# Dots and sums of fetched expert rows, issued on VectorE in the program's order

## The chip, the cores and the metric

The kernel runs on one core of a Trainium2 chip. The metric is the device time of one execution in microseconds (us). The kernel before took 3069.17 us, the median of three runs (3067.21 to 3079.47).

## The reference

The kernel computes a two-layer backbone over 256 latent tokens and 256 context tokens of width 1024. A layer mixes tokens (gated linear attention and neighbourhood attention, merged by gates) and then channels. The channel mixing is what the change touches. It is a retrieval of single-neuron experts (PEER): each token scores 8 heads x 2 x 128 keys, and each head picks 16 of the 16384 experts, so a token has 128 experts in all.

```python
def block(xb):                                # 128 tokens
    ...                                       # qb, s, top 16, cand, top 16: experts, g
    u = jnp.take(expert_u, experts, axis=0)   # (tokens, 128, 1024)
    v = jnp.take(expert_v, experts, axis=0)
    act = jax.nn.gelu(jnp.einsum('td,ted->te', xb, u))
    return jnp.einsum('te,ted->td', act * g, v)
```

The last layer gives out the latent stream alone, so the context stream goes through PEER in layer 0 only, while the latent stream does so in both layers.

## The kernel before, in words

**Two ways of PEER.** For the latent stream the kernel computes all 16384 hidden activations densely on TensorE (`hidden`, L325) and multiplies them by a matrix A that holds the gate of each chosen expert and zero elsewhere. `build` makes A in three chunks from one-hot marks: on VectorE oi (L951), oj (L953) and two products oa (L956) for every 8 tokens, on TensorE their products (L964), on ScalarE the copy into A (L966). `scale` multiplies activations by A in place (L1017), and `value` multiplies the result by expert_v (L1051). `peer_prep` (L915 to L931) lays out the indices and gates ahead of the first chunk.

For the context stream of layer 0 the kernel fetches the chosen rows instead. This is `gather`. For each of 128 expert places and both blocks of 128 tokens, an indirect DMA that GpSimd issues (L1173) brings one row of 1024 numbers to each token's partition, first all rows of expert_u, then all of expert_v: 2 x 256 fetches. A fetched u row is multiplied by the token's normed input hN and added up on VectorE (the dots, L1180, in place in the row's buffer gx). After the last dot a gelu and the gates give the coefficients coef. A fetched v row is scaled by its coefficient and added to the running result vsum (the sums, L1189; the first of each block is L1187). At the end vsum is multiplied by a broadcast row (L1194) and added to the context x (L1195), from which layer 1 starts. There are six buffers for fetched rows (gx=6), and the fetch of a row is written four rows ahead of its dot or sum (lead=4).

**The loops and their weaving.** `gather` is a generator that yields after each row; two yields for hN come first. The program runs it in three places beside work on the latent stream. In the mixer of the latent stream it takes five rows at each of 17 steps, after the heads of the context stream are done. In the head stage of the latent stream (query, scores, top 16 of eight heads, with the hidden activations of eight of the 32 groups) it takes three rows at each of ten steps. In `peer_out`, the loop over 32 groups of 512 experts, it takes 400/224 rows at each of the 224 steps. An iteration of that loop scales the group's activations, computes the hidden activations of the group four further on (four steps, in iterations 4 to 27) and the value products (four steps). The second and third chunk of A are built beside iterations 4 to 7 and 16 to 19. What is left of `gather` is run ahead of iteration 31.

**What sets the order.** The kernel is written on a tile framework that fixes each engine's order of instructions when the program is built. It plays the program through with times of its own for instructions and transfers, and on each engine it issues what is ready by then, the earliest in the program first. On the chip each engine takes its instructions in that fixed order and waits, where an operand isn't there yet, at the instruction that needs it. Dots and sums are free in this: one whose row has come, by those times, is issued ahead of VectorE work that stands before it in the program and isn't ready. The order of fetches on GpSimd's queue is the program's, and a fetch waits until one of the six buffers is free. Weights are loaded by SP into four buffers (w) and two more (dw), a tile of 512 KB each.

The method `keep_in_program_order` of the framework takes an instruction and adds an edge to it: it is issued after the instruction of its engine that the program wrote just before it. The edge is one of order; it adds no semaphore and no wait for an end. Instructions that the program writes later may still be issued ahead of it.

Of the kernel before, what the change touches and what calls it, by code (L numbers as in the profile page):

```python
# [17 lines left out]
OP = mybir.AluOpType  # L18
# [51 lines left out]
class Net:  # L70
# [1073 lines left out]
    def gather(self, l, s, st):  # L1144


        nc, gp = self.nc, self.gp
        si = 0 if s == "l" else 1
        n, lead = self.n["gx"], self.n["lead"]
        sh, sc = (self.modT[l][:, 24 + 8 * i:32 + 8 * i, si] for i in range(2))  # L1150
        g = gp.tile([128, 8], F32, name="gcol", bufs=1)
        nc.vector.scalar_tensor_tensor(g, sc, 1.0, self.colv[f"gn2{l}"], op0=OP.add, op1=OP.mult)
        rows = [self.wtile([128, D]) for i in range(2)]
        for row, col in zip(rows, (g, sh)):
            self.row_of([row[:, 0:512], row[:, 512:D]], col)
        def room(name):
            return [self.pe.tile([128, D], F32, name=name, tag="hp", bufs=self.n["hp"]) for b in range(2)]
        hN, sums = room("hn"), None
        for b in range(2):
            nc.vector.scalar_tensor_tensor(hN[b], self.x[s, b], self.rs[s][:, b:b + 1], rows[0], op0=OP.mult, op1=OP.mult)  # L1160
            nc.vector.tensor_tensor(out=hN[b], in0=hN[b], in1=rows[1], op=OP.add)
            yield
        idx = st["idx"].rearrange("p b h r -> p b (h r)")
        coef = gp.tile([128, 2, 128], F32, name="coef", bufs=1)
        nr = 128
        jobs = [(w, b, r) for w in "uv" for r in range(nr) for b in range(2)]
        tabs = {w: self.t["expert_" + w].rearrange("l e d -> (l e) d") for w in "uv"}
        got = []
        for i in range(len(jobs) + lead):
            if i < len(jobs):  # L1170
                w, b, r = jobs[i]
                x = gp.tile([128, D], F32, name="gx", bufs=n)
                nc.gpsimd.indirect_dma_start(x, None, tabs[w], bass.IndirectOffsetOnAxis(ap=idx[:, b, r:r + 1], axis=0),  # L1173
                                             element_offset=l * NK * NK * D)
                got.append(x)
            if i >= lead:
                w, b, r = jobs[i - lead]
                x = got.pop(0)
                if w == "u":
                    nc.vector.tensor_tensor_reduce(out=x, in0=x, in1=hN[b], scale=1.0, scalar=0.0, op0=OP.mult, op1=OP.add,  # L1180
                                                   accum_out=coef[:, b, r:r + 1])
                    if (r, b) == (nr - 1, 1):
                        nc.scalar.activation(coef, coef, AF.Gelu_apprx_tanh)
                        nc.vector.tensor_tensor(out=coef, in0=coef, in1=st["g"].rearrange("p b h r -> p b (h r)"), op=OP.mult)
                elif r == 0:
                    sums = sums or room("vsum")
                    nc.vector.tensor_scalar(sums[b], x, coef[:, b, 0:1], None, op0=OP.mult)  # L1187
                else:
                    nc.vector.scalar_tensor_tensor(sums[b], x, coef[:, b, r:r + 1], sums[b], op0=OP.mult, op1=OP.add)  # L1189
            yield  # L1190
        ga = self.wtile([128, D])
        self.row_of([ga[:, 0:512], ga[:, 512:D]], self.modT[l][:, 40:48, si])
        for b in range(2):
            nc.vector.tensor_tensor(out=sums[b], in0=sums[b], in1=ga, op=OP.mult)  # L1194
            nc.vector.tensor_tensor(out=self.x[s, b], in0=self.x[s, b], in1=sums[b], op=OP.add)  # L1195
            for h in range(2):
                hs = slice(h * 512, (h + 1) * 512)
                self.square(s, b, h, self.x[s, b][:, hs], sums[b][:, hs])
            self.dump(f"xp{l}{s}{b}", self.x[s, b])
            yield  # L1200
        self.root(s, 2)
        yield
# [151 lines left out]
```

## Time and profile before

| what | us |
|---|---|
| median of the runs | 3069.17 |
| the profiled execution | 3073.63 |
| its span, first to last instruction | 3071.9 |
| TensorE matmul busy | 2785.7 (91%) |
| VectorE busy | 2164.1 (70%) |
| ScalarE busy | 978.1 (32%) |
| GpSimd busy | 612.6 (20%) |
| mean granted clock of TensorE | 0.951 of full |

The profile is of one execution. Its busy times are of one engine over the span; they overlap. The idle time before an instruction is given with what released it, inferred from semaphores. A wait costs the kernel only where the waiting engine holds up the end. GB/s and the DMA share are of the core's 16 DMA engines; a share near 1.0 means that they have no pause. "DVE" is VectorE, "PE" TensorE, "PEld" its weight loads, "ACT" ScalarE, "POOL" GpSimd.

### The profile page before, as it was taken

The numbers are of one execution on the slowest core, as the hardware profiler recorded it, in microseconds if no ns is written. First come the engines' busy times: TensorE is split into PE (matmuls) and PEld (weight loads), VectorE is DVE, ScalarE is ACT, GpSimd is POOL, SyncE is SP. The second block draws the span as 40 slices with busy tenths as digits, with TensorE's granted clock in tenths as the row PEclk, the third lists the DMA queues.
The fourth block names the chain that finished last, engine by engine and source line by source line (L and its number), as shares of the span: only waits on it lengthen the run. The fifth ranks groups of instructions, "written<-read, shape, count | busy, mean of one in ns | idle before, by whom it ended". The sixth has DMA issues, their size and how long they took to land.

```text
span 3071.9 us, 45729 instructions
## 1 busy us (share of the span) xinstructions
PE 2785.7 (91%) x17380; PEld 2239.8 (73%) x17380; DVE 2164.1 (70%) x4525; ACT 978.1 (32%) x1798; POOL 612.6 (20%) x528
## 2 busy tenths in 40 slices
PE   7999999977984899995699999899988999999998
PEld 3779787756873466663466665898988889998987
DVE  3656676767999698667996204576699989548755
ACT  4454212301113021000120004545533556446544
POOL 0000000254432576445764000000000000000000
PEclk8999999988995999998899999999998999999999
DMA  7564655699984999999999654444443455665564
GB/s 262 185 201 138 222 184 169 222 373 365 336 292 145 373 385 401 409 409 387 355 384 409 204 154 130 120 123 131 155 151 121 132 180 164 190 189 164 178 196 148
DMA packets 295707, 724.64 MB, mean 236 GB/s; under 512 B 26816, under 2 KB 147904, under 8 KB 295488
## 3 DMA queue, kind: packets, MB, share of 16 engines
q1 hardware_dynamic: 221760, 453.25, 45.0%
q0 software_dynamic: 73728, 268.47, 22.7%
q8 instruction: 137, 2.24, 0.3%
q14 instruction: 82, 0.67, 0.1%
HBM read 720.58 MB, written 1.05 MB: 235 GB/s over the span
## 4 chain that ended last, share of the span: by engine, by line
PE 41%; DVE 10%; DMA 9%; issue 6%; POOL 2%; ACT 1%; DVEq 0%; POOLq 0%; ACTq 0%
PE ps L1051 17%; DMA gx<-in_expert_v,idx 8%; PE ps L328 5%; PE ps L330 5%; PE ps L329 5%; PE ps L325 4%; POOL gx L1173 2%; DVE gx L1180 1%; DVE vsum L1189 1%; PE ps L964 1%; DMA gx<-in_expert_u,idx 1%; DVE wlo L148 1%; DVE eid L885 1%; DVE oi L951 1%; DVE oa L956 1%
## 5 line engine op out<-in xcount | busy, mean ns | idle before, releaser
L148 DVE TENSOR_TENSOR wlo<-w,whi 128x1024 fp32r<-128x1024 f32 (+1 forms) x404 | 487.8, 1208 | 255.8 <-ACT whi L215 254.7
L215 ACT ACTIVATE whi<-w 128x1024 fp32r<-128x1024 f32 (+1 forms) x404 | 421.9, 1046 | 471.0 <-PE ps L329 276.7
L1173 POOL DMA_INDIRECT gx<-in_expert_u,idx x256 | 317.3, 1239 | 832.0 <-DVE ga_y L499 341.5
L325 PE MATMUL ps<-hph,w 128*128 128x256 f32 x1888 | 429.8, 386 | 9.2 <-DMA w<-in_w_query 9.2
L325 PEld LDWEIGHTS ps<-hph,w 128*128 128x128 f32 x1888 | 363.0, 194 | 69.8 <-issue 16.3
L1189 DVE SCALAR_TENSOR_TENSOR vsum<-gx,coef,vsum 128x1024 f32<-128x1024 f32 x254 | 324.9, 1285 | 121.7 <-DMA gx<-in_expert_v,idx 121.1
L330 PE MATMUL ps<-hph,wlo 128*128 128x256 f32 x1152 | 329.9, 287 | 21.7 <-DVE wlo L148 21.7
L1180 DVE CUSTOM_DVE_ANT_0 gx<-gx,hn 128x1024 f32<-128x1024 f32 x256 | 310.9, 1222 | 52.8 <-DMA gx<-in_expert_u,idx 51.5
L328 PE MATMUL ps<-hph,whi 128*128 128x256 f32 x1152 | 334.2, 290 | 2.7 <-ACT whi L215 2.5
L329 PE MATMUL ps<-hpl,whi 128*128 128x256 f32 x1152 | 329.1, 286 | 0.0
L1173 POOL DMA_INDIRECT gx<-in_expert_v,idx x256 | 283.7, 1108 | 219.4 <-DVE vsum L1189 149.8
L1051 PE MATMUL ps<-w,A 128*128 128x512 f32 x680 | 302.7, 595 | 0.0
L966 ACT ACTIVATE A<-ps 128x128 f32<-128x128 f32 x512 | 144.2, 425 | 325.5 <-PE ps L964 325.4
L330 PEld LDWEIGHTS ps<-hph,wlo 128*128 128x128 f32 x1152 | 223.3, 194 | 23.8 <-DVE wlo L148 23.6
L1051 PEld LDWEIGHTS ps<-w,A 128*128 128x128 f32 x680 | 128.2, 190 | 149.1 <-issue 148.2
L328 PEld LDWEIGHTS ps<-hph,whi 128*128 128x128 f32 x1152 | 223.7, 194 | 4.3 <-ACT whi L215 3.3
L329 PEld LDWEIGHTS ps<-hpl,whi 128*128 128x128 f32 x1152 | 223.6, 194 | 0.5
L1001 ACT ACTIVATE act<-ps 128x512 f32<-128x512 f32 x112 | 66.2, 593 | 476.2 <-PE ps L325 445.6
L964 PE MATMUL ps<-oa,oi 128*128 128x48 f16 (+1 forms) x3072 | 113.3, 185 | 101.1 <-DVE oa L956 99.1
L964 PEld LDWEIGHTS <-oi 128*128 128x128 f16 x3072 | 97.2, 99 | 136.5 <-DVE oa L956 107.0
L1051 PE MATMUL ps<-whi,Ah 128*128 128x512 f32 x512 | 160.7, 395 | 0.0
L1051 PE MATMUL ps<-dw,A 128*128 128x512 f32 x344 | 158.9, 605 | 1.3 <-issue 1.3
(283 smaller groups left out, 5048.7 us busy)
## 6 DMA issues: line engine op xcount, KB each, us to landing
w<-in_expert_ut SPq DMA_DIRECT2D x214, 512.0 KB, 4.0
w<-in_expert_v SPq DMA_DIRECT2D x213, 512.0 KB, 3.6
w<-in_w_in SPq DMA_DIRECT2D x134, 512.0 KB, 3.9
w<-in_w_mod SPq DMA_DIRECT2D x96, 512.0 KB, 4.6
w<-in_w_query SPq DMA_DIRECT2D x48, 512.0 KB, 4.2
dw<-in_expert_v SPq DMA_DIRECT2D x43, 512.0 KB, 6.7
dw<-in_expert_ut SPq DMA_DIRECT2D x42, 512.0 KB, 6.8
w<-in_w_out SPq DMA_DIRECT2D x24, 512.0 KB, 3.4
```

The lines of the kernel that those rows point to most:

```text
L148: self.nc.vector.tensor_tensor(out=lo, in0=full, in1=hi, op=OP.subtract)
L215: nc.scalar.activation(hi, w, AF.Copy)
L325: nc.tensor.matmul(ps, wpairs[0], xpair[0], start=first, stop=last, skip_group_check=True)
L328: nc.tensor.matmul(ps, wh, xh, start=first, stop=False, skip_group_check=True)
L329: nc.tensor.matmul(ps, wh, xl, start=False, stop=False, skip_group_check=True)
L330: nc.tensor.matmul(ps, wl, xh, start=False, stop=last, skip_group_check=True)
L964: nc.tensor.matmul(pv[:, u, :], oi[:, u // TU, :, u % TU], oa[:, i, u // TU, :, u % TU], start=(i == 0), stop=(i == 1))
L966: nc.scalar.activation(st["A", s0 + i][:, :, ts].rearrange("p j t -> p t j"), pv[:, :, i * SUB:(i + 1) * SUB], AF.Copy, scale=1.0 / GS)
L1051: nc.tensor.matmul(acc[b, h], aa[:, x, ts], v[x][ww][:, h * 512:(h + 1) * 512], start=(j == 0 and n == 0), stop=(j == NK - 1 and n == len( ...
L1173: nc.gpsimd.indirect_dma_start(x, None, tabs[w], bass.IndirectOffsetOnAxis(ap=idx[:, b, r:r + 1], axis=0), element_offset=l * NK * NK * D)
L1180: nc.vector.tensor_tensor_reduce(out=x, in0=x, in1=hN[b], scale=1.0, scalar=0.0, op0=OP.mult, op1=OP.add, accum_out=coef[:, b, r:r + 1])
L1189: nc.vector.scalar_tensor_tensor(sums[b], x, coef[:, b, r:r + 1], sums[b], op0=OP.mult, op1=OP.add)
```

## The change

Each dot (L1180) and each sum (L1189) is handed to `keep_in_program_order`. The two first scalings L1187, the fetches, the buffers and all other instructions are as they were.

```diff
-        nc, gp = self.nc, self.gp
+        nc, gp, keep = self.nc, self.gp, self.tc.keep_in_program_order
...
                 if w == "u":
-                    nc.vector.tensor_tensor_reduce(out=x, in0=x, in1=hN[b], scale=1.0, scalar=0.0, op0=OP.mult, op1=OP.add,
-                                                   accum_out=coef[:, b, r:r + 1])
+                    keep(nc.vector.tensor_tensor_reduce(out=x, in0=x, in1=hN[b], scale=1.0, scalar=0.0, op0=OP.mult, op1=OP.add,
+                                                        accum_out=coef[:, b, r:r + 1]))
...
                 else:
-                    nc.vector.scalar_tensor_tensor(sums[b], x, coef[:, b, r:r + 1], sums[b], op0=OP.mult, op1=OP.add)
+                    keep(nc.vector.scalar_tensor_tensor(sums[b], x, coef[:, b, r:r + 1], sums[b], op0=OP.mult, op1=OP.add))
```

## Rows read from the trace of the kernel before

**Rows 1.** Busy time by stage: stretch, length, then each engine's us (instructions), clock, DMA share, GB/s.

```profile
core 0: us, PE busy (x) PEld busy (x) DVE busy (x) ACT busy (x) POOL busy (x), PEclk, DMA share, GB/s
758.00:909.00 151.00, 151.00 (x727) 133.73 (x725) 150.46 (x583) 18.96 (x30) 60.93 (x49) 1.00 0.89 324
909.00:938.00 29.00, 0.03 (x1) 0.00 (x0) 29.00 (x80) 2.78 (x4) 17.27 (x14) 0.55 0.74 254
938.00:990.00 52.00, 25.73 (x518) 19.55 (x518) 52.00 (x164) 20.27 (x66) 10.06 (x9) 0.50 0.33 113
990.00:1047.00 57.00, 56.70 (x129) 25.20 (x130) 40.27 (x70) 0.00 (x0) 27.01 (x24) 0.97 0.85 320
1047.00:1194.00 147.00, 130.95 (x898) 88.65 (x897) 136.78 (x281) 31.49 (x104) 103.18 (x76) 0.95 1.00 389
1194.00:1414.00 220.00, 220.00 (x768) 146.20 (x768) 146.22 (x134) 9.97 (x17) 105.95 (x109) 1.00 1.03 408
1414.00:1607.00 193.00, 131.11 (x899) 88.42 (x898) 177.22 (x234) 31.12 (x104) 133.94 (x104) 0.85 0.97 369
1607.00:1707.00 100.00, 100.00 (x361) 68.60 (x360) 64.23 (x54) 4.78 (x8) 43.27 (x45) 1.00 1.02 405
1707.00:1883.00 176.00, 176.00 (x551) 103.28 (x550) 16.91 (x24) 12.49 (x27) 0.61 (x1) 1.00 0.45 138
```

**Rows 2.** The same for instructions on fetched rows (gx) alone: DVE's dots and sums, POOL's fetches.

```profile
0.00:758.00 758.00, 96.21 (x79) 99.38 (x85) 0.95 0.69 231
758.00:909.00 151.00, 59.35 (x49) 60.93 (x49) 1.00 0.89 324
909.00:938.00 29.00, 19.01 (x16) 17.27 (x14) 0.55 0.74 254
938.00:990.00 52.00, 9.05 (x8) 10.06 (x9) 0.50 0.33 113
990.00:1883.00 893.00, 453.75 (x361) 413.35 (x355) 0.96 0.88 337
1047.00:1194.00 147.00, 93.41 (x78) 103.18 (x76) 0.95 1.00 389
1194.00:1414.00 220.00, 135.81 (x107) 105.95 (x109) 1.00 1.03 408
1414.00:1607.00 193.00, 132.10 (x104) 133.94 (x104) 0.85 0.97 369
```

**Rows 3.** TensorE's instructions in order of time: start, length, idle before and its releaser.

```profile
938.79 0.45 PE L919 MATMUL ps<-fc,w 128*128 128x128 f32 x1 [29.75 <-DVE w L915]
...
1069.36 1.02 PE L964 MATMUL ps<-oa,oi 128*128 128x48 f16 x16 [10.93 <-DVE oa L956]
...
1481.31 1.02 PE L964 MATMUL ps<-oa,oi 128*128 128x48 f16 x16 [55.61 <-DVE oa L956]
...
1548.18 0.80 PE L964 MATMUL ps<-oa,oi 128*128 128x48 f16 x16 [2.29 <-DVE oa L956]
```

**Rows 4.** Groups by line, 990 to 1883: count, busy and mean, idle before and its releasers.

```profile
L1189 DVE SCALAR_TENSOR_TENSOR vsum<-gx,coef,vsum 128x1024 f32<-128x1024 f32 x254 | 324.9, 1285 | 121.7 <-DMA gx<-in_expert_v,idx 121.1
...
L964 PE MATMUL ps<-oa,oi 128*128 128x48 f16 x1024 | 38.7, 185 | 77.9 <-DVE oa L956 77.1
```

**Rows 5.** VectorE's instructions in order of time, at the end of TensorE's longest wait.

```profile
1477.81 2.57 DVE L1189 SCALAR_TENSOR_TENSOR vsum<-gx,coef,vsum 128x1024 f32<-128x1024 f32 x2 [0.24 <-DMA gx<-in_expert_v,idx]
1480.30 0.68 DVE L951 TENSOR_TENSOR oi<-io,iT 128x1024 f16<-128x1024 f16 x1
```

**Rows 6.** Busy time of two short stretches, columns as in the first group.

```profile
716.00:758.00 42.00, 29.05 (x122) 24.70 (x123) 26.59 (x50) 5.21 (x10) 20.27 (x20) 0.82 1.03 396
1541.00:1553.00 12.00, 9.02 (x81) 7.60 (x82) 10.55 (x20) 1.86 (x8) 5.52 (x5) 1.00 0.96 380
```

**Rows 7.** Order of time: the last sum, the end of the gather, the start of layer 1.

```profile
1706.87 1.28 DVE L1189 SCALAR_TENSOR_TENSOR vsum<-gx,coef,vsum 128x1024 f32<-128x1024 f32 x1 [1.42 <-DMA gx<-in_expert_v,idx]
...
1870.10 2.36 DVE L1194 TENSOR_TENSOR vsum<-vsum,w 128x1024 f32<-128x1024 f32 x2 [55.16 <-ACT w L232]
...
1885.87 2.12 PE L272 MATMUL ps<-fc,xs 128*128 128x128 f32 x16 [1.88 <-DVE rs_l L261]
```

## The prediction, made before the change was run

> **What bounds the kernel now.** I read the busy times by stage first, those of all engines beside those of the instructions that touch a fetched row [rows 1, 2]. The change concerns the 512 rows per token block (256 dots, then 256 sums) of layer 0's context stream. Until 758 us the mixer runs beside them. From 758 to 909 TensorE is full (151.00 of 151 us) with hidden activations and head queries of the latent stream; VectorE is full too, 59.35 us of it with 49 row dots. From 909 to 938 TensorE does nothing (0.03 us) while VectorE works all 29.00 us, 19.01 of them on 16 dots. From 938 to 990 VectorE is full again and TensorE follows it with 25.73 of 52. Then comes the loop of `peer_out`, 990 to 1883: TensorE is full from 1194 to 1414 and from 1607 on, but busy only 130.95 of 147 and 131.11 of 193 in two stretches between. After 1883 nothing of the change runs.
>
> The waits of TensorE, read next in its order of time, name the places [rows 3]: 29.75 us at 938.79 for L915, the start of `peer_prep`; 10.93 us at 1069.36 and 55.61 us at 1481.31 for L956, a mark product of `build`. The groups by line put 77.1 us of waiting for L956 on the loop [rows 4]. VectorE's own order shows why [rows 5]: two sums at 1477.81, the last of a train that waits row by row, and then L951 at 1480.30, the mark that TensorE had been waiting for. So rows that are worked on early cost TensorE time in two places: ahead of the loop by the VectorE time they take, in the loop by their place in its queue.
>
> DMA is the other limit: from 1194 to 1414 its share is 1.03 at 408 GB/s, with TensorE still full [rows 1].
>
> **The change part by part.** It adds and removes no operation; it moves up to 510 (the two of L1187 stay free). Each dot or sum goes behind the VectorE instruction that the program has just ahead of it.
>
> *Where the rows go.* Beside the mixer stand 17 x 5 steps of `gather`; two make hN and four are the lead, so 79 dots stand there, and 10 x 3 = 30 more in the head stage: 109. The next one stands behind the first scaling L1017 of the loop, which needs the first chunk of A. Now 79 dots are done at 758, as many as are due, so up to there next to nothing moves; and 361 of the 512 are left for the loop [rows 2], so 512 - 361 - 79 = 72 run between (49 + 16 + 8 in its parts, one at a border counted twice). The program has 30 there: 42 must leave.
>
> *Ahead of the loop.* From 758 to 938 the program has 30 dots where 65 run, so 35 x 1.21 us (59.35 / 49) = 42 us come off VectorE ahead of L915, which TensorE now awaits until 938.79 [rows 3]. It would be ready at 897, sooner than TensorE, which is full to 909. So the 29 us idle go, and TensorE is late next. From there to the loop VectorE has 52.00 - 9.05 = 43 us of work that isn't rows [rows 1, 2], hence loop start at 909 + 43 = 952 instead of 990: 38 us less. Bounds: 939, if all 42 x 1.21 = 51 us come off, and 990.
>
> *The loop.* It has 32 iterations: four with value products alone, 24 with hidden and value, four with value alone; two chunks are built beside iterations 4 to 7 and 16 to 19. The stretch 1194 to 1414 is eight full ones (768 matmuls, 96 each). Rows are dealt out at 400/224 a step, eight steps to a full iteration: 14.3. Now 361 rows are left for the loop; then 403. In the build iterations dots and sums stand between the marks, so a mark has one or two rows ahead of it, no train: the 55.61 and the 10.93 go. What is late next is DMA. A row is 128 x 1024 x 4 bytes = 0.524 MB, a weight tile the same, so a full iteration moves 22.3 x 0.524 = 11.7 MB, at 408 GB/s in 28.6 us, where TensorE needs 220 / 8 = 27.5 [rows 1]. The 1.1 us return as waits, collected where a mark or scaling stands behind a late sum. The sum: four iterations 57 (as now); build 131 (TensorE's busy time there, 130.95); eight iterations 8 x 28.6 = 229; build 131; eight more 229; the last four 56: 833 us, where 893 stand now, 60 less. VectorE covers the build steps: marks and scalings take (136.78 - 93.41) / 32 = 1.36 us of a step, 1.79 rows take 1.79 x 93.41 / 78 = 2.1, together 3.5, beside TensorE's 131 / 32 = 4.1. If that cover fails, rows and marks take turns: 1.79 x 220 / 107 = 3.7 for rows that wait for DMA, and 1.36: 5.0 a step, 30 us more for each build, 893. The other bound is 815, TensorE's busy time summed from 990 to 1883. I take 833, nearest to the stretch 1047 to 1194, where 78 dots passed between marks and 57 will stand.
>
> *The end.* Now the last sum is at 1706.87, and L1194 waits 55.16 us for a broadcast row that TensorE makes late; from it to the first transpose of layer 1 are 1885.87 - 1870.10 = 16 us [rows 7]. With rows up to the last iteration, this chain can stand alone: 0 to 16 us, I take 8.
>
> *POOL and SP.* The fetches are not pinned, but each needs one of six buffers, which a dot or sum frees: between the last heads and 952 they pause, and DMA idles where nothing else asks for it; that is why 403 rows are left. SP's weight loads lose a competitor there and gain one from 1707 to 1883, where the share is now 0.45 [rows 1].
>
> Sum: -38 - 60 + 8 = -90 us against the profiled execution, 3073.63 us (the span of 3071.9 and 1.7 around it): 2984. The median of the runs, 3069.17, is 4.5 lower, so 2979; I say 2980.
>
> **The rivals.** *A, more.* The lag of the rows hides in the slack of the scalings (act is four iterations ahead): loop 815, start 939 to 952, 2948 to 2961 or, with no chain at the end, 2940. For it: TensorE full at saturated DMA from 1194 to 1414. Against: 403 rows and 224 weight tiles are 329 MB, 806 us at 408 GB/s, which leaves little slack.
>
> *B, gain eaten by turns.* The pinned row makes VectorE wait for DMA and then DMA for VectorE, as in the upper bound: loop 893, start 952: -38 + 8 = -30, 3039; with a later start, no change. For it: 121.1 us of waits for rows stand before the sums now [rows 4], and marks will queue behind them. Against: in 1414 to 1607, 104 rows passed in 193 us beside the marks [rows 2].
>
> *C, slower: the clock.* One long wait becomes many short ones. From 716 to 758, where TensorE was busy 29.05 of 42 us, its granted clock was 0.82; from 1541 to 1553, with a wait of 2.29 in it, it was 1.00 [rows 3, 6]. If the waits of a DMA-bound loop grow to the former kind, all 833 us run slower: the gain is gone when the mean granted clock of the loop falls below 833 / 923 = 0.90, and at 0.82 the loop takes 1016 us: 3069 - 90 + 183 = 3162. Against: 1.1 us an iteration is short, and the 1.00 is the nearer row. The Trainium skill, TensorE: Matmul & The Clock Gate, section HAM oscillation, tells of such a kernel: each tile's products are shorter than the wait for the next transfer, so the engine falls back to half clock and starts every tile cold. By that rule the time would be C's; the rows here show the fall beside long waits only.
>
> *D, slower: the tail.* If the planned order puts marks and scalings far ahead of the sums, rows are left when TensorE has finished; each then costs about a sum's 1.28 us, plus 16 for the chain. It decides from (98 - 16) / 1.28 = 64 rows on, over four iterations of lag; 100 rows give 3069 - 98 + 144 = 3115. For it: nothing holds a scaling behind the sums. Against: the last sum now comes when TensorE is in iteration 23 of 31, so sums are ready early.
>
> *E, nothing moves.* Excluded for the 42 dots, which can't stand ahead of L1017; in time it is B with a start near 990.
>
> **How the numbers follow.** Forecast (2960 to 3015) 0.53, A 0.08, B up to 3054 0.13, no change (the rest of B, and E) 0.09, C 0.08, D 0.09. Half a per cent, 15 us, is about what a measurement here tells from none. Faster 0.74, same 0.09, slower 0.17. The range of 8 in 10 runs from 2940, which takes in A, to 3075, which takes in B and no change; C and D stay outside.
>
> **What would show it.** Right: the 110th dot starts after the first L1017; TensorE's idle stretch at 909 shrinks under 10 us; the loop starts near 952, takes about 833 us at a DMA share near 1.0 and a clock of 0.95 or more, with no wait for L956 over 10 us; rows go on until some 30 us before its end. Wrong: a start at 980 or later (VectorE's other work bound it, not the dots); a wait of tens of us for L956 or L1017 (the train has only moved); sums after the last L1051 (D); a clock below 0.9 in the loop (C).

## The result, and the profile after

The changed kernel takes 2997.18 us, the median of four runs (2996.47 to 2997.39), against 3068.74 for the kernel before in the same comparison: a ratio of 0.9759, 95% interval 0.9737 to 0.9781. It is 72 us faster; forecast were 89, with 2980. The profiled execution took 2997.31 us, its span is 2995.5, 76.4 less than before.

The stages come first, in the windows of the changed kernel: stretch, length, each engine's busy time, clock, DMA share and GB/s. They answer to [rows 1].

```profile
750.00:901.00 151.00, 150.96 (x727) 133.29 (x725) 146.83 (x582) 17.69 (x28) 38.02 (x33) 1.00 0.79 270
901.00:912.00 11.00, 0.00 (x0) 0.00 (x0) 10.83 (x22) 3.76 (x6) 2.44 (x2) 0.62 0.27 83
912.00:957.00 45.00, 25.85 (x518) 19.60 (x518) 44.21 (x150) 20.46 (x66) 1.16 (x2) 0.50 0.13 41
957.00:1014.00 57.00, 56.89 (x128) 25.16 (x129) 43.13 (x76) 0.00 (x0) 34.59 (x28) 0.96 0.92 354
1014.00:1154.00 140.00, 127.75 (x898) 86.63 (x897) 116.20 (x246) 30.87 (x104) 80.83 (x60) 0.96 0.93 345
1154.00:1375.00 221.00, 221.00 (x772) 146.28 (x771) 147.44 (x195) 9.75 (x17) 105.70 (x107) 1.00 1.03 409
1375.00:1514.00 139.00, 127.58 (x896) 86.84 (x895) 123.75 (x188) 30.75 (x104) 91.15 (x63) 0.95 0.95 360
1514.00:1735.00 221.00, 221.00 (x771) 146.29 (x770) 149.06 (x127) 9.56 (x16) 109.46 (x109) 1.00 1.03 409
1735.00:1808.00 73.00, 59.22 (x144) 26.16 (x142) 55.93 (x52) 7.87 (x21) 33.16 (x33) 0.93 0.85 328
```

The same view for instructions on fetched rows alone, as in [rows 2]: dots and sums of VectorE, fetches of GpSimd.

```profile
0.00:750.00 750.00, 88.16 (x73) 92.43 (x79) 0.95 0.68 229
750.00:901.00 151.00, 39.08 (x33) 38.02 (x33) 1.00 0.79 270
901.00:912.00 11.00, 3.51 (x3) 2.44 (x2) 0.62 0.27 83
912.00:957.00 45.00, 0.00 (x0) 1.16 (x2) 0.50 0.13 41
957.00:1808.00 851.00, 503.46 (x403) 453.06 (x397) 0.98 0.98 380
1154.00:1375.00 221.00, 132.74 (x108) 105.70 (x107) 1.00 1.03 409
```

The gain is in two places. The loop starts at 957 instead of 990, and with 403 rows in it instead of 361 it takes 851 us instead of 893. From 912 to 957 no dot runs: the 110th stands behind the loop's first scaling. The idle 29 us of TensorE ahead of the loop have become 11. The stage of the second build, 193 us before, is 139. Given back are 17 us at the end: the last four iterations have 36 rows beside them and take 73 us instead of 56.

TensorE's waits in order of time, as in [rows 3]: start, length, idle before and its releaser.

```profile
912.81 0.45 PE L919 MATMUL ps<-fc,w 128*128 128x128 f32 x1 [11.85 <-DVE w L915]
1043.20 0.50 PE L964 MATMUL ps<-oa,oi 128*128 128x48 f16 x3 [9.04 <-DVE oa L956]
1120.32 0.45 PE L964 MATMUL ps<-oa,oi 128*128 128x48 f16 x2 [3.11 <-DVE oa L956]
1397.41 0.58 PE L964 MATMUL ps<-oa,oi 128*128 128x48 f16 x5 [11.17 <-DVE oa L956]
1790.95 8.91 PE L1051 MATMUL ps<-w,A 128*128 128x512 f32 x16 [11.74 <-DVE A L1017]
1810.15 0.56 PE L272 MATMUL ps<-fc,xs 128*128 128x128 f32 x3 [2.43 <-DVE rs_l L261]
```

The wait of 55.61 us has become one of 11.17, the one of 10.93 one of 9.04. The last but one is new, and the rows of VectorE in front of it say what it is:

```profile
1777.30 1.31 DVE L1189 SCALAR_TENSOR_TENSOR vsum<-gx,coef,vsum 128x1024 f32<-128x1024 f32 x1 [1.07 <-DMA gx<-in_expert_v,idx]
1779.43 1.28 DVE L1189 SCALAR_TENSOR_TENSOR vsum<-gx,coef,vsum 128x1024 f32<-128x1024 f32 x1 [0.82 <-DMA gx<-in_expert_v,idx]
1781.35 8.94 DVE L1189 SCALAR_TENSOR_TENSOR vsum<-gx,coef,vsum 128x1024 f32<-128x1024 f32 x7 [0.64 <-DMA gx<-in_expert_v,idx]
1790.21 0.69 DVE L1017 TENSOR_TENSOR A<-act,A 128x512 f32<-128x512 f32 x1
...
1796.19 2.35 DVE L1194 TENSOR_TENSOR vsum<-vsum,w 128x1024 f32<-128x1024 f32 x2
```

That is a train of sums again, ahead of iteration 31's scaling. 220 steps of 400/224 rows bring 392 of the 403, and the program runs what is left ahead of iteration 31: eleven rows. The chain from L1194 to layer 1 [rows 7] lies beside the last products, as it did before: its last instruction on VectorE runs at 1804.52, with products of iteration 31 behind it. The 2.43 us that layer 1 waits are for the root of the latent stream (rs_l), as the 1.88 before were.

```profile
1804.52 0.17 DVE L261 RECIPROCAL rs_c<-rs_c 128x2 f32<-128x2 f32 x1 [0.33 <-ACT rs_c L260]
```

From there on the two kernels take about the same (changed 1185.35 us, before 1186.03 to the end of the span).

The wait of 9.04 us at 1043.20 is of another kind. The mark in front of it, L951 at 1042.18, stands behind one dot, and that dot waits for its row:

```profile
1041.03 1.23 DVE L1180 CUSTOM_DVE_ANT_0 gx<-gx,hn 128x1024 f32<-128x1024 f32 x1 [6.55 <-DMA gx<-in_expert_u,idx]
```

The groups by line from 957 to 1808 answer to [rows 4]:

```profile
L1189 DVE SCALAR_TENSOR_TENSOR vsum<-gx,coef,vsum 128x1024 f32<-128x1024 f32 x254 | 323.9, 1285 | 131.8 <-DMA gx<-in_expert_v,idx 131.5
...
L964 PE MATMUL ps<-oa,oi 128*128 128x48 f16 x1024 | 35.8, 185 | 23.7 <-DVE oa L956 23.3
```

Sums still wait for rows, 131.5 us in all, even a little longer; what stands behind them has changed.

### The profile page after: what moved, and what is told of

Read it like the earlier page. It is cut to its first block, busy times and chain, and to the rows that moved or that the text cites. A ratio compares the mean times of both kernels' runs of the same rounds, so it can differ in the third digit from the quotient of the medians.

```text
span 2995.5 us, 45775 instructions
## 1 busy us (share of the span) xinstructions
PE 2781.6 (93%) x17380; PEld 2232.5 (75%) x17380; DVE 2181.6 (73%) x4525; ACT 976.9 (33%) x1798; POOL 598.7 (20%) x528
## 4 chain that ended last, share of the span: by engine, by line
PE 51%; DMA 19%; DVE 18%; issue 7%; POOL 3%; ACT 2%; SPq 0%; DVEq 0%; POOLq 0%; ACTq 0%
PE ps L1051 13%; DMA gx<-in_expert_v,idx 12%; PE ps L325 8%; PE ps L328 7%; PE ps L330 7%; PE ps L329 7%; POOL gx L1173 3%; DVE gx L1180 2%; DVE vsum L1189 2%; DMA gx<-in_expert_u,idx 2%; PE ps L964 2%; DVE eid L885 2%; DVE wlo L148 2%; PE ps L542 1%; PE ps L175 1%
## 5 line engine op out<-in xcount | busy, mean ns | idle before, releaser
L1173 POOL DMA_INDIRECT gx<-in_expert_u,idx x256 | 303.6, 1186 | 914.7 <-DVE coef L1180 514.8
L1189 DVE SCALAR_TENSOR_TENSOR vsum<-gx,coef,vsum 128x1024 f32<-128x1024 f32 x254 | 323.9, 1285 | 131.8 <-DMA gx<-in_expert_v,idx 131.5
L1180 DVE CUSTOM_DVE_ANT_0 gx<-gx,hn 128x1024 f32<-128x1024 f32 x256 | 308.7, 1224 | 89.9 <-DMA gx<-in_expert_u,idx 89.1
L1051 PE MATMUL ps<-wlo,Ah 128*128 128x512 f32 x512 | 158.0, 390 | 0.0
L1051 PE MATMUL ps<-whi,Al 128*128 128x512 f32 x512 | 157.7, 389 | 0.0
```

Source lines behind the costliest of these rows:

```text
L1051: nc.tensor.matmul(acc[b, h], aa[:, x, ts], v[x][ww][:, h * 512:(h + 1) * 512], start=(j == 0 and n == 0), stop=(j == NK - 1 and n == len( ...
L1180: keep(nc.vector.tensor_tensor_reduce(out=x, in0=x, in1=hN[b], scale=1.0, scalar=0.0, op0=OP.mult, op1=OP.add, accum_out=coef[:, b, r:r + 1]))
L1189: keep(nc.vector.scalar_tensor_tensor(sums[b], x, coef[:, b, r:r + 1], sums[b], op0=OP.mult, op1=OP.add))
```

## The experiments

Four numbers are read from each profiled execution: the first L775 of the heads, the first L915, the first product of the loop, and the time from that to the first transpose L272 of layer 1 (called the loop). "Dots" are those between the first L775 and L915; "waits" is TensorE's idle time in the loop for L956 and L1017.

| kernel | us, median | ratio to before | L775 | L915 | dots | start | rows left | loop | waits |
|---|---|---|---|---|---|---|---|---|---|
| before | 3069 | 1 | 758.4 | 938.4 | 65 | 990.3 | 361 | 895.5 | 77.1 |
| changed | 2997.2 | 0.976 (0.974-0.978) | 750.3 | 912.4 | 36 | 957.1 | 403 | 853.0 | 36.1 |
| 1 dots only | 3038.8 | 0.991 (0.989-0.992) | 753.0 | 915.1 | 36 | 959.8 | 403 | 889.9 | 70.3 |
| 2 sums only | 3024.4 | 0.985 (0.983-0.987) | 758.9 | 939.8 | 65 | 991.6 | 361 | 847.7 | 28.5 |
| 3 loop only | 2986.4 | 0.974 (0.972-0.975) | 757.3 | 907.4 | 30 | 951.8 | 403 | 850.1 | 34.8 |
| 4 half bytes | 2959.9 | 0.964 (0.962-0.966) | 769.5 | 921.6 | 24 | 966.3 | 403 | 809.9 | 0.9 |
| 5 five a step | 2995.9 | 0.975 (0.972-0.977) | 755.2 | 932.5 | 56 | 977.7 | 383 | 837.1 | 20.3 |
| 6 as 3, five | 2990.1 | 0.973 (0.970-0.975) | 761.3 | 926.0 | 50 | 970.6 | 383 | 835.7 | 22.1 |
| 7 as 3, seven | 3009.2 | 0.980 (0.977-0.982) | 753.7 | 942.7 | 70 | 987.3 | 363 | 833.5 | 20.4 |
| 8 mixer free | 2995.3 | 0.975 (0.972-0.977) | 755.2 | 913.4 | 30 | 958.0 | 403 | 853.0 | 34.4 |
| 9 as 3, deal | 2978.9 | 0.971 (0.970-0.972) | 748.6 | 898.8 | 30 | 943.1 | 403 | 847.7 | 22.0 |
| 10 deal | 2987.7 | 0.973 (0.972-0.975) | 753.4 | 915.3 | 36 | 960.0 | 403 | 845.1 | 18.2 |
| 11 as 3, four, deal | 2976.8 | 0.970 (0.968-0.971) | 754.0 | 911.7 | 40 | 956.3 | 393 | 834.8 | 11.9 |
| 12 as 3, five, slow start | 2979.7 | 0.971 (0.969-0.973) | 754.2 | 918.9 | 50 | 963.5 | 383 | 831.7 | 9.1 |

The first L775 lies between 748.6 and 761.3 in the nine whole-row kernels (before among them) whose mixer is free and the same. So a few us of any start are scatter of one execution, and differences are taken from L775 on.

**1 and 2: one edge each.** The edge on the dots alone, or on the sums alone:

```diff
-                    keep(nc.vector.scalar_tensor_tensor(sums[b], x, coef[:, b, r:r + 1], sums[b], op0=OP.mult, op1=OP.add))
+                    nc.vector.scalar_tensor_tensor(sums[b], x, coef[:, b, r:r + 1], sums[b], op0=OP.mult, op1=OP.add)
```

This is kernel 1, against the changed one; kernel 2 takes `keep` from the dot in the same way.

> Only the dots are pinned; the sums are free as before. Theory (two places, two parts: the dots' edge gives the earlier loop start, the sums' edge takes away the long wait at the marks of the second build): loop start 957 +-6 as in the changed kernel, first build about 140, but a wait for L956 of 30 to 60 us comes back in the second build; the whole 3030 to 3050 us. Rival 1 (dots held back are enough: with 403 rows left no train forms): 2995 to 3008. Rival 2 (the gain is the sums' alone): 3060 to 3072.

> Only the sums are pinned; the dots are free as before. Theory: loop start 990 +-6 and the wait of about 11 us at 1069 as before, 361 rows left for the loop; second build 135 to 145 us instead of 193, and the tail up to 17 us shorter than in the changed kernel, since 42 rows fewer are left: 3010 to 3025 us. Rival 1 (dots held back are enough): 3060 to 3072, with a second build of 180 or more. Rival 2 (the start comes of the pinned sums as well): 2997.

Both came in the range of the theory, 3038.8 and 3024.4; only the end of kernel 2, which I expected up to 17 us shorter than the changed kernel's, is as long (75.3 us from iteration 28 to layer 1). With the dots pinned the loop starts early, and the long wait comes back; with the sums pinned L915 is as late as before, and no wait for a mark is over 11. TensorE's waits, first of kernel 1, then of kernel 2:

```profile
1448.05 1.02 PE L964 MATMUL ps<-oa,oi 128*128 128x48 f16 x16 [57.90 <-DVE oa L956]
```

```profile
940.12 0.45 PE L919 MATMUL ps<-fc,w 128*128 128x128 f32 x1 [30.58 <-DVE w L915]
...
1070.82 1.02 PE L964 MATMUL ps<-oa,oi 128*128 128x48 f16 x16 [10.65 <-DVE oa L956]
...
1819.86 9.75 PE L1051 MATMUL ps<-w,A 128*128 128x512 f32 x16 [11.98 <-DVE A L1017]
```

So the start is the dots' and the train is the sums'. The two gains, 30 and 44 us, add up to about the 72 of the change. In kernel 1 the last four iterations lose nothing, in kernel 2 they do: the train ahead of iteration 31 is the price of the pinned sums.

**3 and 8: where the dots are pinned.** In kernel 3 `keep` does nothing until the loop; kernel 8 sets `pin` ahead of the heads instead, so there it does nothing in the mixer alone. Kernel 3:

```diff
+        def keep(x):
+            if self.n.get("pin"):
+                self.tc.keep_in_program_order(x)
...
+            net.n["pin"] = 1
             net.peer_out(0, [("l", sl)], beside=(rows, 400 / 224))
```

> Dots and sums are pinned only while the loop over 32 groups is written; in the mixer and the heads the dots are free. Theory: what holds the dots back is the edge of the 110th behind the first scaling of the loop, so still 109 rows stand ahead of the loop and 403 in it. The dots in the heads may fill the gaps between short dependent instructions again, so L915 comes at 900 to 912 and the loop starts at 944 to 957: 2984 to 2998 us. Rival 1 (the edges in the heads are what frees VectorE there): start 975 to 990, 3015 to 3030. Rival 2 (order in the heads is of no weight): 957 and 2997 within 3.

> Pinned from the heads on, free in the mixer alone. It splits the difference of the changed kernel and the one pinned in the loop alone (L915 at 912 and 907, 2997 and 2986 us). Theory: the dots held back in the mixer are what counts: 79 dots are done again before the first head, 30 stand in the heads, L915 comes 152 to 156 us after the first L775, start 952 to 957, 2986 to 2993 us. Rival (the order in the heads makes the difference): L915 159 or more after the first L775, 2994 to 3000.

Still 109 dots stand ahead of the loop in kernel 3, so the edges in the loop are what holds them back. L915 comes 150.1 us after L775, where TensorE is full for as long, and TensorE waits 0.2 us for L915 instead of 11.85; 2986.4 us. With 30 dots pinned in the heads (kernel 8) it takes 158.2, nearer to the rival (159) than to the theory (152 to 156), and 2995.3 us is in the rival's range: with as many dots, pinning them in the heads costs 8 us of this stage. Over the whole kernel the intervals of such pairs overlap, but the difference has one sign in all three: kernel 3 is 10.7 us below the changed one, 6 is 5.8 below 5, 9 is 8.8 below 10. In the loop VectorE's order is the same instruction for instruction in the changed kernel, 3 and 8.

**4: half the bytes.** Every fetch brings 512 numbers, VectorE reads them twice (the dot, not shown, reads `half` in the same way).

```diff
-        tabs = {w: self.t["expert_" + w].rearrange("l e d -> (l e) d") for w in "uv"}
+        tabs = {w: self.t["expert_" + w].rearrange("l e (x d) -> (l e x) d", x=2) for w in "uv"}
...
-                nc.gpsimd.indirect_dma_start(x, None, tabs[w], bass.IndirectOffsetOnAxis(ap=idx[:, b, r:r + 1], axis=0),
+                nc.gpsimd.indirect_dma_start(x[:, 0:512], None, tabs[w], bass.IndirectOffsetOnAxis(ap=idx[:, b, r:r + 1], axis=0),
...
+                two = lambda y: y.rearrange("p (a n) -> p a n", a=2)
+                half = x[:, None, 0:512].to_broadcast([128, 2, 512])
...
-                    keep(nc.vector.scalar_tensor_tensor(sums[b], x, coef[:, b, r:r + 1], sums[b], op0=OP.mult, op1=OP.add))
+                    keep(nc.vector.scalar_tensor_tensor(two(sums[b]), half, coef[:, b, r:r + 1], two(sums[b]), op0=OP.mult, op1=OP.add))
```

> The changed kernel with every fetch at half its bytes (512 of 1024 numbers; VectorE reads them twice, so its instructions keep their size, and the output is not the reference's). Theory (what is left of waits in the loop, 36 us at L956 and L1017, is the lag of rows on DMA): these waits fall under 8 us in all, the loop takes 812 to 822 us instead of 851; the mixer, whose weights wait at a DMA share of 1.0 from 600 to 750, ends 5 to 20 us sooner; the whole 2935 to 2962 us. Rival (the waits come of VectorE's turns between rows and marks, whatever the transfer): loop 840 or more, waits of 25 or more left, 2975 or more.

The loop fell to 809.9 us, somewhat under the range; waits for L956 and L1017 are gone but for 0.9; the whole, 2959.9, is in the range. The mixer did not end sooner (769.5), against what I expected; of that nothing more is known. The windows of this kernel, from the first build on:

```profile
1023.00:1163.00 140.00, 139.00 (x958) 97.35 (x957) 121.55 (x255) 31.03 (x105) 89.66 (x63) 1.00 0.77 253
1163.00:1385.00 222.00, 222.00 (x818) 147.26 (x817) 154.93 (x204) 12.45 (x27) 134.12 (x113) 1.00 0.84 287
1385.00:1500.00 115.00, 115.00 (x809) 76.63 (x808) 106.80 (x166) 28.39 (x95) 83.75 (x56) 1.00 0.79 259
```

VectorE does as much beside the marks as in the changed kernel (a sum takes 1286 ns, there 1285), and TensorE is full at 1.00. So what is left in the changed kernel's loop, 853.0 - 809.9 = 43 us, goes with the rows' transfer and not with their turns with the marks. One thing moved along with the bytes: the plan was made with the smaller transfers, and VectorE's order in this loop is not the changed kernel's (30 rows and not 22 stand ahead of the loop's first L956). Which part of the 43 us that order has was not tried. Of the 43, 36 are idle time of TensorE and 7 its matmuls, which are busy 813.4 us in the changed loop, 806.1 here, where the clock stays at 1.00. From the first products of iterations 0, 4, 8, 16, 20 and 28 to L272, the changed kernel takes 73.0, 138.1, 235.9, 124.2, 206.6 and 75.3, half bytes 72.6, 124.8, 222.2, 123.5, 208.1 and 58.7: 13 us are at the first build, 14 in iterations 8 to 15 with the wait of 11.17 in front of the second, 17 at the end.

**5, 6 and 7: more rows in the heads.** Five rows a step in the changed kernel (5), five and seven in kernel 3 (6, 7).

```diff
-            run(net.by_head(net.peer_heads(0, "l", sl)), (net.hiddens(0, sl, 8), 3), itertools.islice(takes(rows, 3), 10))
+            run(net.by_head(net.peer_heads(0, "l", sl)), (net.hiddens(0, sl, 8), 3), itertools.islice(takes(rows, 5), 10))
```

> The changed kernel with five instead of three rows at each of the ten steps in the heads: 129 rows ahead of the loop, 383 left for it. Theory (VectorE sets L915, a pinned dot costs there its whole 1.14 us from start to start, and each row less in the loop saves 1.28 us of DMA time, 0.524 MB at 409 GB/s): L915 at 935, loop start 980, loop 825; the whole 2990 to 2998 us, no gain over the changed kernel. Rival 1 (the loop's waits are not the rows' lag): loop 845 or more, 3010 to 3025. Rival 2 (dots fill gaps for nothing): start 957 to 962, 2970 to 2978.

> The kernel that pins in the loop alone, with five rows at each of the ten steps in the heads. Theory: free dots fill gaps between short dependent instructions (0.28 us of other work saved for each, from 120 us of other work at 36 dots pinned and 106 at 64 free), so one more costs 0.86 us; start 952 + 17 = 969, loop 847 - 26 = 821; 2972 to 2982 us, the fastest so far by 0.2 to 0.5%. Rival 1 (no gap filling): start 975 to 980, 2984 to 2990. Rival 2 (waits of the loop stay): 2998 to 3006.

> The same with seven rows a step: 149 ahead of the loop, 363 in it. Theory: start 952 + 34 = 986, loop not under the 808 that half the bytes gave, so 808 to 815: 2978 to 2990 us, the optimum passed. Rival (the heads' VectorE is not the limit, or the loop gains on): 2960 to 2974.

L915 and the start came near the forecast (932.5, 926.0; starts 977.7, 970.6, 987.3), the loop did not: 837.1, 835.7 and 833.5, where 825, 821 and 808 to 815 were forecast. So kernel 5 was in its range although its loop was 12 us too long, and 6 and 7 were too slow by 8 and 19. Taken from L775 on, L915 was luck in kernel 5: twenty more pinned dots took 177.3 - 162.1 = 15.2 us, 0.76 each and not 1.14, and a later L775 made up the rest. Twenty rows fewer save the train at the end (16.6 us), twenty more save nothing: the loop deals out the same 1.786 rows a step until there are none, so the waits at the builds stay (8.89 and 9.35 in kernel 6). That took the form "a row less saves 1.28 us" down. My next theory was that the wait at a mark belongs to the stretch ahead of it.

**9 to 12: another deal.** Rows a step by kind of iteration (first four, build, full, last four) in place of 400/224: 1.8, 2.1, 1.7, 1.8 in kernel 3 (9) and in the changed kernel (10); 1.75, 2.05, 1.65, 1.75 with four rows a step in the heads (11); the same with 1.0 at first and five rows in the heads (12).

```diff
-                x[2] += x[3]
+                x[2] += x[3] if isinstance(x[3], float) else x[3](now[0])
...
-            net.peer_out(0, [("l", sl)], beside=(rows, 400 / 224))
+            net.peer_out(0, [("l", sl)], beside=(rows, lambda i: 1.8 if i < 4 or i > 27 else 2.1 if i // 4 in (1, 4) else 1.7))
```

> The kernel pinned in the loop alone, with rows dealt out by what each kind of iteration leaves of DMA: 1.8 a step in the iterations with value products alone, 2.1 beside a build, 1.7 in the full ones (1.786 everywhere so far); 403 rows in the loop as before. Theory (a wait at a mark or scaling is the lag that the stretch before it gathered, rows asked for minus rows that DMA brings, and not a matter of the loop's total): the waits of 10.3 at the second build and 13.9 at the end fall under 4 each, the one of 9.2 at the first build may stay; loop 826 to 834 instead of 850, 2960 to 2970 us. Rival (VectorE fills the build steps: 2.1 x 1.2 + 1.36 = 3.9 of 4.1 us): builds of 145 us or more, 2980 to 2995 us.

> The changed kernel, pinned everywhere, with the same deal of rows. Theory: the loop gains as much, the start stays 957: 2971 to 2981 us, 11 behind its sister. Rival: loop 848 to 853 still, 2993 to 3000.

> Pinned in the loop alone, four rows a step in the heads (119 ahead, 393 in the loop), dealt 1.75, 2.05 and 1.65 a step. Theory: start 961, all waits of the loop under 5, loop 818 to 828: 2962 to 2974 us, about as much as with three rows a step. Rival (lag is the loop's total): 10 us below the sister with three rows, 2950 to 2960.

> Pinned in the loop alone, five rows a step in the heads (129 ahead, 383 in the loop), dealt 1.0 a step in the first four iterations, then 2.05 beside a build, 1.65 in the full ones and 1.75 at the end. It asks what the waits at the first build are (9 to 12 us in every kernel but the one with half the bytes, 8.8 in the one with 1.75 a step). Theory (rows and weights of the first iterations together are more than DMA brings once it has started again at the loop's start, so the first mark stands behind late rows): with 12 rows fewer asked for by then, waits at L956 in the first build under 3 us in all, iterations 4 to 7 in 125 to 130 us (136 to 141 so far), loop 818 to 826, 2970 to 2982 us. Rival (marks and rows on VectorE's queue, whatever the deal before): iterations 4 to 7 in 135 or more, loop 833 or more, 2985 to 2995.

Kernel 9: the end's wait fell from 13.9 to 3.57, the second build's only from 10.3 to 7.97, and the loop to 847.7 from 850.1, not to 830; the rest of what it gains on kernel 3 goes with an L775 8.7 us earlier in the profiled execution, which the edit can't have moved. Its 2978.9 us lie over the forecast 2960 to 2970. In kernel 10 the loop is 8 us shorter, but the intervals of its time and the changed kernel's overlap, and 2987.7 us is in neither range: not settled. Kernel 11 met the waits (none over 3.81) but not the loop, 834.8 against 818 to 828, nor the forecast 2962 to 2974; at 2976.8 us (2973.98 to 2976.91) it has the lowest median of the kernels with whole rows (kernels 9 and 12 overlap with it), and its ratio, 0.9696 (0.9682 to 0.9709), lies under the changed kernel's whole interval. Its waits in the loop:

```profile
1036.66 1.02 PE L964 MATMUL ps<-oa,oi 128*128 128x48 f16 x16 [2.54 <-DVE oa L956]
1046.36 0.80 PE L964 MATMUL ps<-oa,oi 128*128 128x48 f16 x16 [3.81 <-DVE oa L956]
...
1399.47 0.80 PE L964 MATMUL ps<-oa,oi 128*128 128x48 f16 x16 [2.55 <-DVE oa L956]
1447.03 2.08 PE L1051 MATMUL ps<-dw,A 128*128 128x512 f32 x2 [3.09 <-DMA dw<-in_expert_v]
```

Kernel 12 has less waiting at the first build (12.2 us in the changed kernel, 7.4 here, in four waits instead of two), yet iterations 4 to 7 took 137.1 us, as ever: neither the theory (125 to 130) nor the rival (waits as before) holds. These iterations are 11 to 16 us longer than at half the bytes in every kernel with pinned sums and dots. In kernel 12 the windows split that: first kernel 12, then half bytes, iterations 4 to 7.

```profile
1037.00:1174.00 137.00, 129.29 (x836) 86.27 (x833) 110.76 (x230) 28.23 (x95) 81.54 (x61) 0.96 0.95 353
1039.00:1164.00 125.00, 124.00 (x834) 84.32 (x834) 109.22 (x229) 28.24 (x96) 83.87 (x60) 1.00 0.79 256
```

Some 7 of the 12 us are idle time of TensorE, and 5 are the same matmuls taking longer, at a granted clock of 0.96 against 1.00. In the changed kernel the same comparison gives 11 and 2. So the shorter waits saved 4 us of idle time and lost most of it again in longer matmuls. Why rows are late here with 12 fewer asked for stays open.

## Why the prediction was right, and where it was not

The direction, the two places and the order of size were right: kernels 1 and 2 show each by itself. The forecast of 2980 was 17 us low. Two of its own signs were missed: TensorE's idle time ahead of the loop is 11.85 us and not under 10, and one wait for L956 is 11.17.

- *Rows' places.* 403 left for the loop, no dot between 912 and 957: as said. But "up to there next to nothing moves" was wrong by six: pinned behind mixer instructions, 73 dots and not 79 are done by the first L775, so 36 stand in the heads and not 30. Kernel 8 undoes that, 79 and 30. (The 512 rows are those of both token blocks together, not of each.)
- *Ahead of the loop: -38 forecast, -33 measured, of which 8 came with an earlier L775, in the scatter: luck.* The failed step is the price of a dot, "35 x 1.21 us come off", and with it that pinning costs nothing. From L775 to L915 it was 180.0 us with 65 dots and is 162.1 with 36: 0.62 us for each, half its duration. Two things are in that. With free dots the stage takes 189.0 us at 70 (kernel 7), 180.0 at 65 (before), 164.7 at 50 (kernels 6 and 12) and 157.7 at 40 (kernel 11), so a free dot less gave 1.2 us from 70 to 50 and 0.7 from 50 to 40; and pinning the dots that stay took some of it back, 8 us at 30 dots (kernels 3 and 8). VectorE's rows show why. First the kernel before, where instructions of two heads and a dot alternate (start, length):

```profile
838.64 0.20 DVE L778 MAX8 best<-mr 128x8 f32<-128x50 f32 x1
838.76 1.21 DVE L1180 CUSTOM_DVE_ANT_0 gx<-gx,hn 128x1024 f32<-128x1024 f32 x1
...
839.89 0.09 DVE L779 MATCH_VALUE_LOAD pos<-best,mr 128x8 f32 x1
...
845.36 0.28 DVE L777 MATCH_REPLACE8 mr<-topv,scr 128x128 f32<-128x128 f32 x1
845.55 0.28 DVE L775 MAX8 topv<-scr 128x8 f32<-128x128 f32 x1
845.75 0.28 DVE L778 MAX8 topv<-mr 128x8 f32<-128x128 f32 x1
```

Then the changed kernel, where L777, L778 and L779, each in need of the one before, stand alone:

```profile
839.14 0.28 DVE L779 FIND_INDEX8 topi<-topv,mr 128x8 uint32<-128x128 f32 x1
839.34 0.16 DVE L887 CAST idx<-eid 128x32 int32<-128x32 f32 x1
...
839.54 0.28 DVE L777 MATCH_REPLACE8 mr<-topv,scr 128x128 f32<-128x128 f32 x1
839.85 0.29 DVE L778 MAX8 topv<-mr 128x8 f32<-128x128 f32 x1
840.18 0.09 DVE L779 MATCH_VALUE_LOAD topi<-topv,mr 128x8 f32 x1
```

An instruction of 0.28 us lets an unrelated one start 0.19 to 0.20 later (845.36, 845.55, 845.75; 839.14, 839.34), one that needs its result 0.31 to 0.33 later (839.54, 839.85, 840.18). The free dots, and the other order around them, had filled such gaps. Summed from start to start, the work that isn't dots, 533 instructions in both, takes 121 us in the changed kernel and 106 before. So L915 came at 912 and not at 897, and TensorE kept 11.85 us of idle time. From there to the loop it was 45 us, where the prediction has 43.
- The Trainium skill, VectorE: DVE Perf Modes, section The DRAIN you can't avoid, says that an instruction which isn't held starts before the pipeline is empty. The trace agrees: the next one starts 0.20 us after the start of one of 0.28.
- *The loop: -60 forecast, -42 measured (893 to 851).* The failed step is where DMA's lag was put. Stage by stage, the eight full iterations took 221 us each where 229 were forecast, the builds 140 and 139 where 131 were, and the last four 73 where 56 were. In the full iterations TensorE is full with 771 matmuls, as before: the lag does not slow them, it is collected where a mark or scaling stands behind late rows. "The 55.61 and the 10.93 go" failed with it: 11.17 and 9.04 stayed. The builds had been put at TensorE's busy time, with no wait in them. 18 us over the no-lag 815 were forecast, and 43 over the 810 of half bytes are paid. The first build's 13 and the 17 of the eleven rows ahead of iteration 31 were not in the sum.
- *The end: +8 forecast, 0 measured.* The chain hides beside iteration 31. The 16 us read from [rows 7] were not a chain that stands alone: before, too, TensorE was full beside it (13.99 of the 14 us from 1870 to 1884).
- *Rivals.* A (loop 815): only half the bytes gave that, 809.9. B (turns, builds 30 us longer and a loop of 893): did not come, the builds took 140 and 139 and the loop 851. C (clock): 0.98 over the loop, so its 1016 us did not come. But the granted clock falls to the lower of its two levels (1.2 of 2.4 GHz) at each of the three long waits, 0.50 to 0.53 in the windows below, where TensorE had been idle, and the 16 matmuls behind the wait of 11.74 take 8.91 us where four take 1.88 later. Its price is within the 7 us that the loop's matmuls are busy longer than with half bytes. The Trainium skill's rule from the prediction (TensorE: Matmul & The Clock Gate, section HAM oscillation) has the clock fall at the wait for each next transfer; the trace agrees with the fall, at three waits of 9 to 12 us in 851. D (tail): the sums end at 1796, ahead of the last product, but the eleven rows left ahead of iteration 31 are its small brother.

```profile
1037.00:1057.00 20.00, 13.76 (x77) 6.81 (x78) 14.98 (x34) 2.53 (x9) 8.12 (x6) 0.75 0.78 269
1037.00:1047.00 10.00, 3.76 (x20) 2.12 (x21) 5.97 (x12) 0.83 (x3) 2.55 (x2) 0.50 0.69 253
1389.00:1402.00 13.00, 4.55 (x25) 3.74 (x26) 11.72 (x17) 0.83 (x3) 7.54 (x5) 0.50 0.72 276
1784.00:1795.00 11.00, 4.05 (x6) 1.75 (x7) 11.00 (x11) 0.00 (x0) 4.62 (x5) 0.53 0.85 333
```

In the first of these windows, around the changed kernel's first wait for a mark, the DMA share falls to 0.78 too. SP issues no weight load there from 1034.1 to 1049.2. My reading, not tried, is that the weight tiles stay in their buffers while TensorE stops, so that the loads pause and DMA time is lost just when rows are late.

## What to carry to other kernels

On an in-order engine the price of background work is what stands behind it: keep it in the program's order where other engines wait for marks (the loop), and leave it free where it fills gaps between short dependent instructions (the heads). Price moved work by the stretch with and without it, not by its duration: here 29 instructions of 1.21 us less, and the rest held in order, made the stage shorter by 0.62 us for each. When a background stream is at DMA's limit, look where its remainder is drained, and let its deal end ahead of the last instruction that someone waits for: that was 17 of 43 us. Look at the matmuls' busy time as well as at the waits: the shorter waits of kernel 12 saved idle time and lengthened the matmuls between.

## What was not expected of the hardware

- Dependent short VectorE instructions start 0.32 us apart where unrelated ones of the same length start 0.20 apart.
- At a DMA share of 1.03 and 409 GB/s TensorE stayed full for 221 us, twice, while the loop as a whole took 43 us less with half the rows' bytes: the limit showed only at the marks and scalings.
- The same mixer, in nine executions of kernels that differ later only, reached its end between 748.6 and 761.3 us.
